# Values as the stationary operand of the attention's second product, for two query tiles at once, with feature-major results, weights spread through DRAM and merges behind the late gate

## The chip, the cores and the metric

The kernel runs on one core of a Trainium2 chip. TensorE (PE) multiplies; each multiplication has a weight load (PEld) that puts its stationary operand into the array, and a matmul that streams its moving operand through. VectorE (DVE), ScalarE (ACT) and GpSimd (POOL) do the elementwise work, and SyncE (SP) issues nearly all transfers. The metric is device time in microseconds: 1720.42 us is the median of three runs before (1719.05 to 1720.85).

## The reference, cut to what matters

One decoder block on a sequence of 1024 tokens of width 1024:

```
h = rms_norm(x);  z = h @ w_in            # q, k, v, GLU input, two gates
for each of 3 groups (dilation 1, 4, 16), 8 heads of 64:
    s = q k^T / 8 + bias(distance), masked to a causal window of 128 steps
    o_g = softmax(s) v;   lse_g = logsumexp(s)
y_attn = (sum over g of softmax_g(lse) * o_g) @ w_attn_out
y_conv = silu(layer_norm(conv31(glu))) @ w_conv_out
x += rms_norm((sig(ga) * y_attn + sig(gc) * y_conv) @ w_mix_out)
x += rms_norm(swiglu(rms_norm(x)))
```

The change concerns the second product of the attention (softmax weights times values) and the merge of the three groups with softmax weights over lse.

## The kernel before, in words

All products are done in three passes over a high and a low part of each operand: hi*hi, hi*lo, lo*hi. A float32 tile is split by a cast on ACT (high part) and a subtraction on DVE or POOL (low part).

**Order of the stages** (times of the profiled execution). Up to 112 us: normalisation and the first GLU blocks. From 112 to 551 us: `winograd` (lines 326 to 361) does 23 pairs of channel blocks, each as seven products with weight combinations A11, A12, S1 to S4 and A22, in the order A11, A12, S2, S1, S3, S4, A22. `prod` (lines 314 to 324) emits a product: 12 matmuls on lines 321 (hi*hi), 322 (hi*lo) and 323 (lo*hi), and one tick after each three. The bank X collects A11, S2, S3 and A22; lines 335, 340 and 345 copy banks out on ACT between the products, and a product that adds onto a bank follows the copy. `quarters` (lines 199 to 234) makes the combinations at fixed ticks of the pair, its parts c = 0 to 5: `both` (lines 193 to 197) casts on ACT (195) and subtracts on POOL (196); c = 1 and 3 add on POOL (215, 216, 222, 223); c = 4 splits S3/S4 with `both`; c = 5 casts on ACT (231) and subtracts on POOL (232) for A22. Line 706 adds up finished convolution channels on POOL, lines 650 to 695 are the convolution on DVE and POOL. From 551 us: the value projections `v` (lines 925 to 966, matmuls 948, 950, 952), and beside them the normalisation of the convolution. From 616 to 870 us the attention runs beside them, then beside the late gate (`plain_gate` with job `late`) and the first conv-out units (lines 1507 to 1526). Then the rest of conv-out, the attention output projection, the mix product (line 1585), and the FFN, whose first product is again `winograd` and whose second is line 1856.

**How the attention is interleaved.** `attention` is a generator. `beat`, called after each matmul of the stages beside it, adds RATE (0.42 beside the values, 0.8 beside late gate and conv-out) and advances the generator for each whole credit. One step s does `att_s` (first product and bias of query tile s), `att_e` (exponential of s-1), `att_t` (transposes of s-LT with the identity, then high and low copies on ACT and DVE), and `att_p` (second product of s-LP). There are 96 steps: 12 pairs of heads by 8 query tiles. `tick` advances background generators (`merge`, `conv_split`, `out_parts`, conv_norm) that say by `yield n` how many ticks to skip. Instructions stand on every engine and on the SP queue in the order in which this Python emits them, and every engine works in that order.

**The second product.** `att_p` holds the transposed weights stationary, high then low part, and streams the values: 128 columns (high and low part, line 1107), then 64 (high part, line 1109), for each key block and head. A DVE reduction (line 1115) adds the two halves into a token-major tile O. Groups 0 and 1 store O to DRAM; group 2 keeps it.

**The merge.** One for each pair of heads: two loads, the softmax over the groups, three multiplications by weights that DVE reads spread over 64 columns, two additions, and eight transposes on PE (line 1166) to feature-major. The first two merges run beside the value projections and go through DRAM (`out_parts`); the last two wait until the attention is done.

**Buffers.** SBUF tiles come from rings of buffers with a tag: 42 slots of 4 KB a partition (tag b), 11 halves of 2 KB (c), 3 ring tiles (d). A tile takes a buffer whose former tile is released, and its first write waits for that tile's last reader. Which buffer a tile gets is settled when the program is built, and the slots are used by all stages.

Of the kernel before, what the change touches and what calls it, by code (L numbers as in the profile page):

```python
# [9 lines left out]
F32 = mybir.dt.float32  # L10
# [36 lines left out]
NSLOT = 42  # L47

NRING = 3
NHALF = 11  # L50
# [12 lines left out]
class Build:  # L63
# [359 lines left out]
    def consts(self):  # L423
        nc = self.nc
        self.ident = self.small.tile([128, 128], F32, name="ident")
        nc.gpsimd.dma_start(self.ident, self.p_ident)
        tab = self.small.tile([33, 24], F32, name="tab")
        nc.gpsimd.memset(tab[32:33, :], 1.0)
        nc.gpsimd.dma_start(tab[0:32, :], self.p_tab)
        self.tab = tab  # L430
        self.mean_col = self.small.tile([128, 1], F32, name="mean_col")
# [457 lines left out]
    def others(self, hp):  # L889

        outs = [self.slot(), self.slot()]
        for i, o in enumerate(outs):
            self.nc.sync.dma_start(o.rearrange("p (u e) -> p u e", u=8),
                                   self.d_att[i, hp].rearrange("(p u) e -> p u e", u=8))
        return outs

# [19 lines left out]
    def value_parts(self, x, i):  # L916

        v = self.slot(F32R)
        d = v.rearrange("p (t e c) -> p t e c", t=8, e=2)
        y = x[:, i * H:(i + 1) * H].rearrange("p (t c) -> p t c", t=8)  # L920
        self.nc.scalar.copy(d[:, :, 0], y)
        self.nc.gpsimd.tensor_tensor(d[:, :, 1], y, f(d[:, :, 0]), op=OP.subtract)
        return v
# [45 lines left out]
    LT, LP = 3, 4  # L969
# [3 lines left out]
    def attention(self):  # L973
# [10 lines left out]
        while s < total + self.LP:  # L984
            if s < total:
# [22 lines left out]
                if u in (3, 4):  # L1008
                    if len(V) < 2:
                        V.append(self.value_parts(x, u - 3))  # L1010
                    if u == 4:
                        x = None
# [15 lines left out]
            if 0 <= s - self.LT < total:  # L1028
                self.att_t(live[s - self.LT])
                yield 0  # L1030
            if 0 <= s - self.LP < total:
                yield from self.att_p(live.pop(s - self.LP))
# [44 lines left out]
    def att_t(self, a):  # L1077

        nc = self.nc
        nb = len(a["blocks"])  # L1080
        ps = self.bank("t")
        for hh in range(2):
            for kb in range(nb):
                i = hh * nb + kb
                nc.tensor.transpose(ps[:, i * 128:(i + 1) * 128],  # L1085
                                    a["sp"][:, hh * 256 + kb * 128:hh * 256 + (kb + 1) * 128], self.ident)
        a["sp"] = None
        n = 2 * nb * 128
# [3 lines left out]
        a["pt"] = hi, lo  # L1092

    def att_p(self, a):

        nc = self.nc
        g, hp, u, nb = a["g"], a["hp"], a["u"], len(a["blocks"])
        ps = self.bank("o")
        hi, lo = a["pt"]
        for hh in range(2):  # L1100
            o = hh * 128
            for i, kb in enumerate(a["blocks"]):
                kb = self.place(g, kb)
                c = (kb % 4) * 256 + hh * 128
                v = a["V"][kb // 4]
                s = slice((hh * nb + i) * 128, (hh * nb + i + 1) * 128)
                nc.tensor.matmul(ps[:, o:o + 128], hi[:, s], v[:, c:c + 128], start=i == 0, stop=False,  # L1107
                                 skip_group_check=True)
                nc.tensor.matmul(ps[:, o:o + 64], lo[:, s], v[:, c:c + 64], start=False, stop=i == nb - 1,  # L1109
                                 skip_group_check=True)  # L1110
            yield 0
        if u == 0:
            self.O = self.ring() if g < 2 else self.slot()
        w = self.place(g, u)
        nc.vector.tensor_reduce(self.O[:, w * 128:(w + 1) * 128].rearrange("p (h c) -> p h c", h=2),
                                ps[:, :256].rearrange("p (h e c) -> p h c e", h=2, e=2), AX.X, OP.add)
        if u == 7:
            if g < 2:
                self.tokens_out(g, self.d_att[g, hp], self.O.rearrange("p (u e) -> p u e", u=8))
            else:  # L1120
                self.merges.append(self.bg(self.merge(hp, a["p"][4], self.O)))
            self.O = None

    def merge(self, hp, st, last):


        nc = self.nc

        late = 1 + (hp > 1)
        while hp > 1 and (self.fine is not None or hp > len(self.OT) + 2):  # L1130
            yield 0
        O = [*self.others(hp), last]
        last = None
        yield 1 + late
        t = self.tiny(96, "mrg", 2)
        m, r = (t[:, i * 16:(i + 1) * 16].rearrange("p (u e) -> p u e", u=8) for i in range(2))
        w = t[:, 48:].rearrange("p (g u e) -> p g u e", g=3, u=8)
# [3 lines left out]
        nc.scalar.activation(t[:, 48:], t[:, 48:], AF.Exp, scale=-1.0)  # L1141
        yield late
# [3 lines left out]
        nc.vector.tensor_tensor(w, w, r.unsqueeze(1).to_broadcast([128, 3, 8, 2]), op=OP.mult)  # L1146
        for g in range(3):
            y = O[g].rearrange("p (u h c) -> p u h c", u=8, h=2)
            a = w[:, g].unsqueeze(3).to_broadcast([128, 8, 2, 64])
            nc.vector.tensor_tensor(y, y, a, op=OP.mult)  # L1150
            yield late
        nc.vector.tensor_tensor(O[1], O[1], O[2], op=OP.add)
        O[2] = y = a = None
        yield late
        nc.vector.tensor_tensor(O[0], O[0], O[1], op=OP.add)
        O[1] = None
        yield 2 + 2 * late
        if hp < 2:
            hi = self.slot()
        else:  # L1160
            hi, lo = self.slot(F32R), self.slot(F32R)
        for h in range(2):
            ps = self.bank("t")
            for i in range(4):
                u = h * 4 + i
                nc.tensor.transpose(ps[:, i * 128:(i + 1) * 128], O[0][:, u * 128:(u + 1) * 128], self.ident)
            y = ps.rearrange("p (u m) -> p u m", u=4)
            a = hi.rearrange("p (m u) -> p u m", u=8)[:, h * 4:h * 4 + 4]
            nc.scalar.copy(a, y)
            if hp > 1:  # L1170
                nc.vector.tensor_tensor(lo.rearrange("p (m u) -> p u m", u=8)[:, h * 4:h * 4 + 4], y, f(a),
                                        op=OP.subtract)
            ps = y = a = None
            yield late
        if hp > 1:
            self.OT[hp] = hi, lo
        else:
            self.nc.sync.dma_start(self.d_ot[hp], hi)

    def out_parts(self):  # L1180

        for hp in range(2):
            x = self.slot()
            self.nc.sync.dma_start(x, self.d_ot[hp])
            yield 11
            self.OT[hp] = self.both(x)
            x = None
# [67 lines left out]
    def conv_split(self):  # L1255
# [11 lines left out]
        for i in range(16):  # L1267
# [3 lines left out]
            yield 3 if i < 5 else 1  # L1271
            while i == 5 and self.hH is not None:
                yield 0
# [71 lines left out]
def build(ctx, tc, aps):  # L1345
# [40 lines left out]
    B.d_att = {(g, hp): B.dram.tile([T, 128], F32, name=f"datt{g}{hp}") for g in range(2) for hp in range(4)}  # L1386
    B.d_v = {(g, hp): B.dram.tile([T, 128] if g else [128, T], F32, name=f"dv{g}{hp}") for g in range(3) for hp in range(4)}
    B.d_ot = [B.dram.tile([128, 1024], F32, name=f"dot{p}") for p in range(2)]
# [118 lines left out]
    for n, hf in [(0, 0), (1, 0), (0, 1), (1, 1)] + [(n, hf) for n in range(2, 8) for hf in range(2)]:  # L1507
# [20 lines left out]
    B.finish(op)  # L1528
# [443 lines left out]
```

## Time and profile before

| | |
|---|---|
| median of three runs | 1720.42 us |
| profiled execution | 1720.29 us |
| its span, first to last instruction | 1718.5 us |
| granted TensorE clock, mean | 0.999 |
| PE / PEld / DVE / ACT / POOL busy | 1700.9 / 1449.9 / 1235.5 / 794.2 / 461.4 us |
| moved by DMA | 277.03 MB, mean 161 GB/s |
| share of PE in the chain that ended last | 95% |

A profile row names the line, engine, operation and the tiles as out<-in without buffer numbers: p is a PSUM bank, b a slot, c a half, d a ring tile, others are DRAM tensors. Matmuls overlap, so their durations add up to more than their time; the distance from start to start is what one costs in a stream. In a timeline row stand the start, the length, and in brackets the idle time before it and what ended that. In a row of waits stand the total, the number and the longest.

### The profile page before, as it was taken

To read this page: it belongs to the slowest core of one execution; us is meant where nothing else is said; L and a number is where in the kernel's file an instruction comes from. 1 tells how busy PE (TensorE), PEld (TensorE's weight loads), DVE (VectorE), ACT (ScalarE), POOL (GpSimd) and SP (SyncE) were. 2 spreads that over 40 slices of the span, in tenths; PEclk is the share of its full clock that TensorE was granted. 3 is DMA by queue.
4 is the path that set the end of the run, shared out by engine and by line. 5 is a ranking of instruction groups with operands and counts; after the bars stand their busy time and mean duration, and the time that the engine had idled before them with its cause. 6 is when DMAs were issued, how large, how long until landed. Compare 5 with 4: busy or idle time off the path is not lost.

```text
span 1718.5 us, 24444 instructions
## 1 busy us (share of the span) xinstructions
PE 1700.9 (99%) x8698; PEld 1449.9 (84%) x8698; DVE 1235.5 (72%) x2217; ACT 794.2 (46%) x1552; POOL 461.4 (27%) x337
## 2 busy tenths in 40 slices
PE   8999999999999999999999999999999999999998
PEld 7788888888888999999888888888888888888886
DVE  6789978888998566686764855676556555677586
ACT  6344343444344486667722445633333333454463
POOL 0017777887886133342300120000000000000000
PEclk9999999999999999999999999999999999999999
DMA  4252433455568798888845732123222322494234
GB/s 165 103 183 86 151 125 132 152 189 172 172 177 215 214 276 209 243 225 232 277 170 182 257 113 98 68 74 132 108 92 92 127 94 92 145 361 156 97 136 153
DMA packets 169334, 277.03 MB, mean 161 GB/s; under 512 B 51921, under 2 KB 87244, under 8 KB 169212
## 3 DMA queue, kind: packets, MB, share of 16 engines
q1 hardware_dynamic: 168812, 274.97, 49.4%
q8 instruction: 68, 1.11, 0.3%
q14 instruction: 54, 0.44, 0.1%
q10 hardware_dynamic: 288, 0.27, 0.0%
q0 software_dynamic: 112, 0.24, 0.0%
HBM read 184.81 MB, written 95.33 MB: 163 GB/s over the span
## 4 chain that ended last, share of the span: by engine, by line
PE 95%; DMA 2%; ACT 1%; DVE 1%; POOL 1%; issue 0%; DVEq 0%; SPq 0%; ACTq 0%; POOLq 0%
PE p L321 16%; PE p L322 16%; PE p L323 15%; PE p L1856 12%; PE p L305 5%; PE p L309 5%; PE p L307 5%; PE p L1585 5%; PE p L950 2%; PE p L952 2%; PE p L948 2%; PE p L554 2%; PE p L1050 2%; PE p L1085 2%; PE p L1109 1%; PE p L1107 1%
## 5 line engine op out<-in xcount | busy, mean ns | idle before, releaser
L321 PE MATMUL p<-b,b 128*128 128x512 f32 x1204 | 469.1, 390 | 0.3 <-ACT c L340 0.3
L323 PE MATMUL p<-b,b 128*128 128x512 f32 x1204 | 469.0, 390 | 0.0
L322 PE MATMUL p<-b,b 128*128 128x512 f32 x1204 | 468.9, 389 | 0.0
L321 PEld LDWEIGHTS p<-b,b 128*128 128x128 f32 x1204 | 226.1, 188 | 48.1 <-ACT c L340 0.7
L323 PEld LDWEIGHTS p<-b,b 128*128 128x128 f32 x1204 | 226.1, 188 | 46.7
L322 PEld LDWEIGHTS p<-b,b 128*128 128x128 f32 x1204 | 226.1, 188 | 46.6
L1856 PE MATMUL p<-b,b 128*128 128x512 f32 x924 | 209.6, 389 | 0.0
L1856 PEld LDWEIGHTS p<-b,b 128*128 128x128 f32 x924 | 173.5, 188 | 35.9
L684 DVE SCALAR_TENSOR_TENSOR p<-b,par,p 128x511 f32<-128x511 f32 (+14 forms) x232 | 163.5, 739 | 0.0
L305 PE MATMUL p<-b,b 128*128 128x512 f32 x368 | 147.7, 401 | 0.0
L309 PE MATMUL p<-b,b 128*128 128x512 f32 x368 | 146.4, 398 | 0.0
L307 PE MATMUL p<-b,b 128*128 128x512 f32 x368 | 146.2, 397 | 0.0
L195 ACT CAST b<-d 128x1024 fp32r<-128x1024 f32 x86 | 90.4, 1051 | 105.1 <-POOL d L216 55.0
L196 POOL TENSOR_TENSOR b<-d,b 128x1024 fp32r<-128x1024 f32 x44 | 106.8, 2428 | 79.9 <-ACT b L195 72.5
L196 DVE TENSOR_TENSOR b<-d,b 128x1024 fp32r<-128x1024 f32 x42 | 51.3, 1221 | 101.0 <-ACT b L195 101.0
L948 PE MATMUL p<-b,b 128*128 128x256 f32 x384 | 115.5, 301 | 0.0
L950 PE MATMUL p<-b,b 128*128 128x256 f32 x384 | 114.8, 299 | 0.0
L952 PE MATMUL p<-b,b 128*128 128x256 f32 x384 | 114.7, 299 | 0.0
L1193 DVE TENSOR_TENSOR b<-c,b 128x512 fp32r<-128x512 f32 x101 | 71.0, 704 | 38.2 <-ACT b L1192 38.0
L1193 DVE TENSOR_TENSOR b<-b,b 128x512 fp32r<-128x512 f32 x117 | 80.1, 690 | 20.7 <-ACT b L1192 18.8
L1192 ACT CAST b<-b 128x512 fp32r<-128x512 f32 x117 | 72.3, 620 | 45.7 <-PE p L1856 18.0
L1585 PE MATMUL p<-b,b 128*128 128x512 f32 x384 | 89.4, 392 | 0.0
(229 smaller groups left out, 3092.4 us busy)
## 6 DMA issues: line engine op xcount, KB each, us to landing
b<-w_in SPq DMA_DIRECT2D x30, 512.0 KB, 4.9
dk<-c SPq DMA_DIRECT2D x48, 256.0 KB, 2.9
dq<-c SPq DMA_DIRECT2D x48, 256.0 KB, 3.7
b<-dq SPq DMA_DIRECT2D x48, 256.0 KB, 5.9
b<-dk SPq DMA_DIRECT2D x48, 256.0 KB, 6.6
b<-w_fi SPq DMA_DIRECT2D x24, 512.0 KB, 4.9
d<-w_in SPq DMA_DIRECT2D x23, 512.0 KB, 4.0
dqS<-c SPq DMA_DIRECT2D x44, 256.0 KB, 2.1
```

The costliest lines, as they stand in the source:

```text
L196: self.wsplit.tensor_tensor(lo, x, f(hi), op=OP.subtract)
L305: nc.tensor.matmul(ps, hi[:, s], a, start=kt == 0, stop=False)
L307: nc.tensor.matmul(ps, hi[:, s], b, start=False, stop=False)
L309: nc.tensor.matmul(ps, lo[:, s], a, start=False, stop=kt == nk - 1)
L321: nc.tensor.matmul(ps, hi[:, s], a, start=first and kt == 0, stop=False, skip_group_check=True)
L322: nc.tensor.matmul(ps, hi[:, s], b, start=False, stop=False, skip_group_check=True)
L323: nc.tensor.matmul(ps, lo[:, s], a, start=False, stop=kt == 3, skip_group_check=True)
L684: nc.vector.scalar_tensor_tensor(A[i][:, j:], src[i][:, :H - j], w[i], A[i][:, j:], op0=OP.mult, op1=OP.add)
L948: nc.tensor.matmul(o, a, hi[:, s], start=kt == 0, stop=False)
L1193: nc.vector.tensor_tensor(s[:, 512:512 + n], src, f(s[:, :n]), op=OP.subtract)
L1585: nc.tensor.matmul(banks[tt][nh], st, wt[:, nh * H:(nh + 1) * H], start=bool(kt == 0 and a), stop=bool(kt == KT - 1 and b))
L1856: nc.tensor.matmul(acc[t], x, y, start=first and e == 0, stop=last and e == 2, skip_group_check=True)
```

## The change

`att_p` makes the values stationary (64 features and 2 columns more, 66 in all) and streams the transposed weights of two neighbouring query tiles: three matmuls (value high by weight high, value low by weight high, value high by weight low) into one half of a PSUM bank, 256 columns where both tiles attend the block, 128 where one does. The result is feature-major, so DVE copies replace the reductions and all three groups store O to DRAM. A small tile `vx` holds the low part of the last value block. `att_t` transposes for two tiles and one head at a time; LT and LP go from 3 and 4 to 4 and 5. The merge writes its softmax weights to DRAM, loads them spread over 64 partitions (`spread`), multiplies feature-major and splits into parts; its transposes, `out_parts` and `others` go. Merges wait until the input activations are freed (after the late gate) and go one after another (`turn`). `conv_split` waits for the late gate after its fourth split instead of its sixth. The banks for conv-out are taken as soon as the attention is done. Slots go from 42 to 41, halves from 11 to 12.

```diff
-NSLOT = 42
+NSLOT = 41
-NHALF = 11
+NHALF = 12
...
+        self.vx = [self.small.tile([128, 66], F32R, name=f"vx{i}") for i in range(4)]
...
+        w = self.vx[self.vi % 4]
+        self.vi += 1
+        self.nc.gpsimd.tensor_copy(w[:, :64], f(d[:, 7, 1]))
+        return v, w
...
-    LT, LP = 3, 4
+    LT, LP = 4, 5
...
+    def att_t(self, live, k):
+        a, b, hh = live[k & ~1], live[k | 1], k & 1
+        items = [(a, u), (b, u), (a, u - 1), (b, u + 1)]
+        items = [(x, x["blocks"].index(kb)) for x, kb in items if kb in x["blocks"]]
+        ps = self.bank("t")
+        for j, (x, i) in enumerate(items):
+            c = hh * 256 + i * 128
+            nc.tensor.transpose(ps[:, j * 128:(j + 1) * 128], x["sp"][:, c:c + 128], self.ident)
...
+    def att_p(self, live, k):
+        if g == 2:
+            todo = [(u, 0, 128, 0), (u + 1, 128, 128, 128)]
+        else:
+            n = 256 + 128 * (len(a["blocks"]) > 1)
+            todo = [(u, 0, 256, 0)] + [(u - 1, 256, 128, 0)] * (n > 256) + [(u + 1, n, 128, 128)]
+        for j, (kb, x, n, q) in enumerate(todo):
+            vh = v[:, c:c + 66]
+            vl = v[:, c + 64:c + 130] if c < 896 else w
+            o = ps[0:66, hh * 256 + q:hh * 256 + q + n]
+            for i, (y, z) in enumerate(((vh, hi), (vl, hi), (vh, lo))):
+                nc.tensor.matmul(o, y, z[:, x:x + n], ...)
+            if j < 2:
+                yield 0
...
+        for h in range(2):
+            x = ps[0:64, h * 256:(h + 1) * 256]
+            nc.vector.tensor_copy(d[h * 64:(h + 1) * 64], x if g < 2 else ...)
+        if u == 6:
+            nc.sync.dma_start(self.d_att[g, hp], self.O)
...
+    def spread(self, hp, g):
+        x, d = self.slot(), self.d_w[hp]
+        for e in range(2):
+            self.nc.sync.dma_start(x[e * 64:(e + 1) * 64], bass.AP(
+                tensor=d.tensor, offset=d.offset + (2 * g + e) * T, ap=[[0, 64], [1, T]]))
+        return x
...
+        nc.sync.dma_start(self.d_w[hp].rearrange("f (p u) -> p f u", u=8), ...)
+        yield 6
+        while self.hH is not None or hp > self.turn:
+            yield 0
+        y, x = load(0), self.spread(hp, 0)
+        yield 1
+        z, w = load(1), self.spread(hp, 1)
+        yield 8
+        nc.vector.tensor_tensor(y, y, x, op=OP.mult)
...
+        self.turn += 1
...
+        self.OT[hp] = self.both(y)
...
-            yield 3 if i < 5 else 1
-            while i == 5 and self.hH is not None:
+            yield 3 if i < 3 else 1
+            while i == 3 and self.hH is not None:
...
-        if B.tags["g"] == 2 and B.fine is None and not any(e in B.gens for e in B.merges):
+        if B.tags["g"] == 2 and B.fine is None:
             B.banks(g=6, s=2)
-        if n == 4 and hf == 0:
-            op = B.bg(B.out_parts())
```

More of the change, by code (lines that the diff above doesn't have):

```diff
@@ L1028, in attention @@
             if 0 <= s - self.LT < total:
-                self.att_t(live[s - self.LT])
+                self.att_t(live, s - self.LT)
                 yield 0
             if 0 <= s - self.LP < total:
-                yield from self.att_p(live.pop(s - self.LP))
+                yield from self.att_p(live, s - self.LP)
             s += 1
@@ L1091, in att_t @@
         nc.vector.tensor_tensor(lo[:, :n], ps[:, :n], f(hi[:, :n]), op=OP.subtract)
-        a["pt"] = hi, lo
-    def att_p(self, a):
+        a["pt", hh] = hi, lo
+    def att_p(self, live, k):
         nc = self.nc
[L1097 to L1107, printed above, removed]
-                                 skip_group_check=True)
-                nc.tensor.matmul(ps[:, o:o + 64], lo[:, s], v[:, c:c + 64], start=False, stop=i == nb - 1,
-                                 skip_group_check=True)
-            yield 0
-        if u == 0:
[L1113 to L1121, printed above, removed]
-            self.O = None
@@ L1124, in merge @@
-    def merge(self, hp, st, last):
-        nc = self.nc
[L1129 to L1135, printed above, removed]
+        a, b, hh = live[k & ~1], live[k | 1], k & 1
+        g, hp, u = a["g"], a["hp"], a["u"]
+        if hh == 0:
+            a["o"] = self.bank("o")
+        ps = a["o"]
+        hi, lo = a.pop(("pt", hh))
@@ L1156, in merge @@
[L1156 to L1187, printed above, removed]
+        nc.vector.tensor_tensor(t[:, 96:].rearrange("p (g e u) -> p g u e", g=3, e=2).rearrange("p g u e -> p g u e"), w,
+                                r.unsqueeze(1).to_broadcast([128, 3, 8, 2]), op=OP.mult)
@@ new lines, in merge @@
+        yield 8
+        nc.vector.tensor_tensor(y, y, x, op=OP.mult)
+        x = None
+        x = self.spread(hp, 2)
+        yield 2
+        nc.vector.tensor_tensor(z, z, w, op=OP.mult)
+        w = None
+        w = load(2)
+        yield 2
+        nc.vector.tensor_tensor(y, y, z, op=OP.add)
+        z = None
+        self.turn += 1
+        yield 6
+        nc.vector.tensor_tensor(w, w, x, op=OP.mult)
+        x = None
+        yield 2
+        nc.vector.tensor_tensor(y, y, w, op=OP.add)
@@ L1189, in split @@
+        w = None
+        yield 2
+        self.OT[hp] = self.both(y)
+    turn = 0
     def split(self, src, n):
```

83 lines of the change are left out of this document (48 added, 35 removed).

## The prediction

> **What bounds the kernel now.** I read the page's shares first, then the windows by stage, then the timeline of single matmuls. Three stages matter here: the seven-product stage (112 to 551 us, lines 314 to 361), the attention beside the value projections and the first conv-out units (613 to 870 us), and what follows.
>
> ```profile
> PE 1700.9 (99%) x8698; PEld 1449.9 (84%) x8698; DVE 1235.5 (72%) x2217; ACT 794.2 (46%) x1552; POOL 461.4 (27%) x337
> ...
> 112.00:550.80 438.80, 438.53 (x1934) 362.68 (x1933) 387.53 (x534) 182.72 (x271) 337.28 (x192) 1.00 0.49 152
> ...
> 613.00:802.70 189.70, 187.78 (x1622) 186.88 (x1622) 135.21 (x469) 128.65 (x412) 70.20 (x88) 1.00 0.86 236
> 802.70:870.00 67.30, 64.98 (x429) 57.29 (x427) 47.80 (x167) 45.09 (x151) 19.06 (x22) 1.00 0.75 233
> ```
>
> The columns are the stretch and its length, then busy PE, weight loads, DVE, ACT, POOL, the granted clock, DMA share and GB/s. PE is busy throughout. So a saved PE step comes off the end one for one, and a new PE wait is added one for one. In the attention weight loads are as busy as the matmuls (186.88 of 189.70 us). In the seven-product stage POOL is busy 337 of 439 us, more than anywhere else: 14.7 us of each pair's 19.1 (23 pairs of channel blocks).
>
> What one step of the second product costs:
>
> ```profile
> 720.07 0.28 PE L950 MATMUL p<-b,b 128*128 128x256 f32 x1
> 720.19 0.22 PE L1107 MATMUL p<-b,c 128*128 128x128 f32 x1
> 720.25 0.25 PE L1109 MATMUL p<-b,c 128*128 128x64 f32 x1
> 720.33 0.37 PE L952 MATMUL p<-b,b 128*128 128x256 f32 x1
> 720.53 0.28 PE L948 MATMUL p<-b,b 128*128 128x256 f32 x1
> 720.65 0.28 PE L950 MATMUL p<-b,b 128*128 128x256 f32 x1
> ```
>
> Start to start is the cost, since ends overlap. A 256-column matmul takes 0.12 us (720.53 to 720.65). From 720.07 to 720.53 there are two of those and one pair of lines 1107 and 1109: the pair takes 0.46 - 0.24 = 0.22 us. Its 128 columns stream in 0.06 us (720.19 to 720.25) and its 64 columns cannot take longer, so the pair is bound by two weight loads of about 0.112 us, not by its columns.
>
> **The change, part by part. Second product.** Before: 280 pairs x 0.224 = 62.7 us, which is also the busy time of line 1107's group:
>
> ```profile
> L1107 PE MATMUL p<-b,c 128*128 128x128 f32 x280 | 62.7, 250 | 0.3 <-DVE b L1115 0.3
> ...
> L459 PEld LDWEIGHTS p<-b,tab x6: 82/84/86, 52.1 to 92.2; 33*8 33x8 f32 x6
> ...
> L1107 PEld LDWEIGHTS p<-b,c x280: 186/190/193, 618.8 to 869.6; 128*128 128x128 f32 x140
> ```
>
> After, the values are stationary: 66 columns instead of 128, three matmuls per key block and two query tiles. Counting att_p over 12 head pairs and both heads gives 192 matmuls of 256 columns and 456 of 128 (152 triples). The 256s cost 0.12 each, 23.0 us. For the 128s the unknown is a 66-column load. Loads of 8 and of 128 columns last 84 and 190 ns: 0.88 ns per column, so 66 columns save 55 ns of the 112 and about 57 are left, under the 60 ns that 128 columns stream. Only the 128-column load of the matmul behind each triple is exposed: 60 + 60 + 112 = 232 ns, 152 x 0.232 = 35.3 us. Sum 58.3, a gain of **4.4 us**. Bounds: all 456 at 60 ns gives 50.4 (gain 12.3); all at 112 ns gives 74.1 (loss 11.4). I stay near the first, since the 8-column row shows that loads shrink with columns.
>
> [...]
>
> **Transposes.** att_t keeps its 280 transposes, only grouped by two tiles. The merge's 32 go:
>
> ```profile
> 888.59 0.44 PE p L1166 x4
> ```
>
> Eight groups of four at 0.44 us: **-3.5 us**. Their copies, the 96 reductions on DVE (0.42 us each) against 96 copies from PSUM, the 24 POOL copies of 64 columns and the extra column of merge work lie on engines that are at most 71% busy in the attention (135 of 190 us). They cost nothing there while PE's order has one step of slack between att_t and att_p, which the change keeps (LT 4, LP 5). If that cover goes, the price is the late-gate term below.
>
> **The slot.** NSLOT falls from 42 to 41, and NHALF rises from 11 to 12. Slots are taken by weights, splits and spills in every stage, not in the attention alone. In both built programs the live slots reach the pool's size in the seven-product stage, so there a tile is written into the buffer that was freed last. I laid the buffers of the changed program beside the times of this trace. In 10 of the 23 pairs, the low half of S3/S4 (quarters, c = 4, POOL line 196) gets the buffer that held the high half of S1/S2. Its last reader is the second-to-last matmul (line 322) of the S1 product, and the very next product is S3. One such pair:
>
> ```profile
> 365.09 1.05 ACT L195 CAST b<-b 128x1024 fp32r<-128x1024 f32 x1 [1.98 <-PE p L322]
> ...
> 368.67 0.62 ACT L231 CAST b<-b 128x512 fp32r<-128x512 f32 x1 [2.52 <-POOL b L196]
> 369.19 0.58 ACT L340 COPY c<-p 128x512 f32<-128x512 f32 x1
> ```
>
> ```profile
> 366.23 2.41 POOL L196 TENSOR_TENSOR b<-b,b 128x1024 fp32r<-128x1024 f32 x1 [1.42 <-ACT b L195]
> ```
>
> ```profile
> 370.03 0.39 PE L322 MATMUL p<-b,b 128*128 128x512 f32 x1
> 370.26 0.39 PE L323 MATMUL p<-b,b 128*128 128x512 f32 x1
> 370.48 0.39 PE L321 MATMUL p<-b,b 128*128 128x512 f32 x1
> 370.71 0.39 PE L322 MATMUL p<-b,b 128*128 128x512 f32 x1
> 370.94 0.39 PE L323 MATMUL p<-b,b 128*128 128x512 f32 x1
> ```
>
> Now POOL writes from 366.23 to 368.64, and PE reads the low half at 370.94: 2.3 us to spare. Changed, POOL may start at 370.03 + 0.39 = 370.42, ends at 372.83, and the matmul of 370.94 waits **1.9 us**. ACT stands in line too: line 231's buffer is freed by line 323 at 370.65, its cast and then line 340's copy of the X bank end at about 371.8, and the S3 product, which adds onto that bank, can start only then (370.48 before). That lies inside the 1.9. Ten pairs: 19 us.
>
> What is behind POOL's waiting instruction: lines 232, 196, 215, 216, 706, 196, 222, 223 and the next 196. The row 368.67 shows that ACT's line 231 already waits on that last one for a buffer. The pair after 218 us:
>
> ```profile
> 222.33 1.30 POOL L215 TENSOR_TENSOR d<-b 128x512 f32<-128x512 f32 x1
> 223.71 1.28 POOL L216 TENSOR_TENSOR d<-d,d 128x512 f32<-128x512 f32 x1
> 224.96 2.40 POOL L706 TENSOR_TENSOR b<-b,b 128x1024 f32<-128x1024 f32 x1
> 227.43 2.40 POOL L196 TENSOR_TENSOR b<-d,b 128x1024 fp32r<-128x1024 f32 x1
> 229.79 1.30 POOL L222 TENSOR_TENSOR b<-d,b 128x512 f32<-128x512 f32 x1
> 231.04 1.30 POOL L223 TENSOR_TENSOR b<-d,d 128x512 f32<-128x512 f32 x1
> 233.50 2.41 POOL L196 TENSOR_TENSOR b<-b,b 128x1024 fp32r<-128x1024 f32 x1 [1.16 <-ACT b L195]
> ```
>
> ```profile
> 217.71 0.39 PE L322 MATMUL p<-b,b 128*128 128x512 f32 x1
> ...
> 237.20 0.39 PE L321 MATMUL p<-b,b 128*128 128x512 f32 x1
> ```
>
> POOL starts at 218.10 and runs 2.41 + 1.30 + 2.40 + 1.30 + 1.28 + 2.40 to 229.2. A cast of 1.05 (its buffer is the one line 706 frees), 2.40, 1.30, 1.30, a cast, 2.41: 238.8, where now it is 235.9. Lines 231 and 340 after it end at 240.0; PE, already 1.9 late, is ready at 237.20 + 1.9 = 239.1. So this pair waits 0.9 us more. In seven pairs the buffers give such a wait (0.7 to 1.2 each): I take 1.0, 7 us. Together **+26 us** for the slot. Bounds: 0, if POOL's buffers turn out otherwise; 42, if POOL's 4.2 us of delay in each of the ten reached PE whole. I take the sum of the rows.
>
> In the FFN's second product the same shortage makes 31 first writes wait about 2.2 us:
>
> ```profile
> L1856 PE MATMUL p<-b,b 128*128 128x512 f32 x924 | 209.6, 389 | 0.0
> ```
>
> A split is issued three steps of 12 matmuls ahead, 36 x 209.6 / 924 = 8.2 us, so I price this at nothing. Were that lead used up, each would cost up to 2.2.
>
> **Late gate, loads and merges.** conv_split now holds after its fourth split, and merges start only when hH is freed. So after the late gate four splits stand together, and the eighth's load is issued behind the gate's store:
>
> ```profile
> 828.86 0.34 SPq L1439 DMA_DIRECT2D dgc<-b  x1
> 829.30 1.20 SPq L1262 DMA_DIRECT2D c<-dact  x2
> ...
> 842.11 0.62 ACT L1192 CAST b<-c 128x512 fp32r<-128x512 f32 x1 [2.58 <-DMA c<-dact]
> ...
> PE p L1050 <- DMA b<-dk: 1.6, 2, 1.1
> ...
> PE p L321 <- ACT c L340: 0.3, 1, 0.3
> ...
> c<-dact SPq DMA_DIRECT2D x16, 256.0 KB, 10.0
> dgc<-c SPq DMA_DIRECT2D x14, 256.0 KB, 2.5
> ```
>
> A DMA of that size lands after 2.5 (gates, stored) to 10 us (these loads). ACT waits in order at that split, and behind it stand attention's exponentials and high-half copies, on which PE waits. Bounds 0 (landed within the slack of one step) and 8; I take **+3**, the size of the wait at 842. The merges add 24 spread loads of 256 KB and four more tile loads and stores; SP sends them between the loads for the last group (b<-dk, c<-rep), so part of the +3 is theirs. By its yields a merge passes the turn every 17 ticks from the first conv-out tick on, so the fourth does at 68 and has its parts at about 82 of the 128 ticks: the attention output projection does not wait. If it had to, the price would be the rest of that merge.
>
> **Sum.** The profiled execution is 1720.29 us (span 1718.5), 0.13 under the median of the three runs. 1720.3 - 4.4 - 3.5 + 26 + 3 = 1741.4.
>
> **Rivals.** *Other side, faster:* the seven-product stage hides the slot. It decides at one point: if the low half's buffer is free 2.3 us earlier, before 368.5 in the pair shown, POOL is done when PE asks. Then 1720.3 - 7.9 + 0 to 3 = 1712 to 1716. For it: POOL is idle 4.4 us per pair. Against it: the idle time stands before the wait and cannot be drawn forward past a buffer that PE holds. *Loads do not shrink:* 456 at 112 ns; +11.4 in place of -4.4 gives 1757. Against it stands the 84 ns row. *The late-gate burst and the spread loads keep the last group waiting:* +8 to +13 instead of +3, 1746 to 1752; for it the 1.1 us wait on b<-dk, against it a DMA share of only 0.75 in the stretch from 802.70.
>
> **How the numbers follow.** My forecast, slower by 12 to 28, has 0.78. The burst rival has 0.06, the loads rival 0.06, and faster 0.08. No change within 0.2% (3.4 us, about what a measurement here can tell) needs the slot to cost just 3 to 8 us: 0.02. Low end: 19 for the slot and nothing for the burst, 1732. High end: slot 28, burst 10, or part of the loads rival: 1754. That leaves the faster case and the loads rival outside.
>
> **What would show it.** In the changed trace, 112 to 551 us should be about 26 us longer with the same matmuls. POOL line 196 would be ended by PE line 322 in about ten places, and PE lines 321 and 323 would wait on ACT line 340 and POOL line 196, where now the one wait is the 0.3 us quoted above. From 613 to 829 us it should be about 7 us shorter, with triples of 232 ns. The prediction is wrong if that first stage keeps its length, or if the 66-column loads follow each other at 110 ns.

## The result and the profile after

The changed kernel takes **1765.91 us** (median; 1765.19 to 1772.44), the kernel before, run beside it, 1720.58 us: a ratio of **1.0274 (95%: 1.0249 to 1.0299)**. It is slower, as forecast, but by 45 us and not by 21: 12 us above the upper end of the range. The profiled execution took 1765.19 us, with a span of 1763.3 us.

The first view is the page's share of busy time, after the change.

```profile
PE 1711.0 (97%) x8754; PEld 1441.2 (82%) x8754; DVE 1253.7 (71%) x2215; ACT 787.1 (45%) x1546; POOL 467.2 (26%) x365
```

PE was busy 99% of a shorter span before, so it now waits. Where, the windows by stage tell (stretch, length, busy PE, weight loads, DVE, ACT, POOL, granted clock, DMA share, GB/s). The stages are the seven products, the attention beside the values, and the stretch from the last value matmul to the attention's end. After:

```profile
112.00:583.20 471.20, 448.82 (x1932) 362.36 (x1931) 392.80 (x536) 182.37 (x272) 336.60 (x192) 0.99 0.46 141
646.30:831.70 185.40, 181.78 (x1657) 180.00 (x1655) 131.00 (x458) 125.72 (x412) 70.52 (x104) 1.00 0.85 230
831.70:913.20 81.50, 70.78 (x460) 57.30 (x459) 62.70 (x179) 44.31 (x147) 21.55 (x28) 0.94 0.87 238
```

The last two stages before (the first is the prediction's row from 112.00, 438.80 us):

```profile
613.80:802.70 188.90, 186.98 (x1616) 186.08 (x1615) 135.21 (x469) 128.06 (x412) 70.20 (x88) 1.00 0.86 236
802.70:869.90 67.20, 64.88 (x428) 57.19 (x426) 47.80 (x167) 45.09 (x151) 19.06 (x22) 1.00 0.75 233
```

So the 44.9 us between the two profiled executions are +32.4 in the seven products, -3.5 in the attention beside the values, +14.3 from there to its end, and +1.7 in all the rest.

**The seven products.** PE's waits from 112 to 583 us, after (total, times, longest):

```profile
PE p L321 <- ACT c L340: 18.2, 16, 1.9
PE p L323 <- POOL b L196: 4.2, 10, 0.4
```

Before, the only wait of this kind was 0.3 us. The pair that the prediction worked out now stands at 384 us. Its matmuls:

```profile
384.67 0.39 PE L322 MATMUL p<-b,b 128*128 128x512 f32 x1
384.90 0.39 PE L323 MATMUL p<-b,b 128*128 128x512 f32 x1
386.48 0.50 PE L321 MATMUL p<-b,b 128*128 128x512 f32 x1 [1.19 <-ACT c L340]
386.82 0.40 PE L322 MATMUL p<-b,b 128*128 128x512 f32 x1
387.63 0.50 PE L323 MATMUL p<-b,b 128*128 128x512 f32 x1 [0.41 <-POOL b L196]
387.97 0.40 PE L321 MATMUL p<-b,b 128*128 128x512 f32 x1
```

and POOL's subtraction, after:

```profile
385.21 2.36 POOL L196 TENSOR_TENSOR b<-b,b 128x1024 fp32r<-128x1024 f32 x1 [4.22 <-PE p L322]
```

POOL sits idle for 4.22 us until line 322 has read the buffer, then takes 2.36 us, and PE reads the low half at 387.63. From 384.90 to 387.97 four matmuls took 3.07 us; at 0.23 each, as in the prediction's rows, they would take 0.92. The pair lost 2.15 us, of which the brackets show 1.60. Idle time understates: in the stream a matmul starts 0.23 us after the one before it, which lasts 0.39, so each of the two waits also loses that overlap of 0.16, and from the matmul behind it to the next start are 0.34 us and not 0.23.

**The second product** moves as the forecast has it. A stretch of it after (x3 is a triple):

```profile
752.73 0.34 PE L1123 MATMUL p<-c,b 128*66 128x128 f32 x3
752.90 0.33 PE L949 MATMUL p<-b,b 128*128 128x256 f32 x1
753.08 0.28 PE L951 MATMUL p<-b,b 128*128 128x256 f32 x1
753.19 0.28 PE L947 MATMUL p<-b,b 128*128 128x256 f32 x1
753.31 0.34 PE L1123 MATMUL p<-c,b 128*66 128x128 f32 x3
```

From 752.73 to 753.31 are a triple and three 256-column matmuls of 0.12: 0.58 - 0.36 = 0.22 us, where I had 0.232. The extra sits behind line 949 (0.18 instead of 0.12); that the wide load of the next matmul is no longer hidden there is my reading of it. The 66-column loads last 136 ns (median, from start to end), close to the straight line between the prediction's 84 ns for 8 columns and 190 ns for 128.

**The end of the attention.** ACT, after, waits here for loads of conv_split:

```profile
861.50 0.62 ACT L1219 CAST b<-c 128x512 fp32r<-128x512 f32 x1 [2.71 <-DMA c<-dact]
...
878.14 0.62 ACT L1219 CAST b<-c 128x512 fp32r<-128x512 f32 x1 [3.07 <-DMA c<-dact]
878.66 0.37 ACT L1095 CAST c<-p 128x256 fp32r<-128x256 f32 x1
...
883.75 0.62 ACT L1219 CAST b<-c 128x512 fp32r<-128x512 f32 x1 [3.17 <-DMA c<-dact]
```

Directly behind the split of 878.14 stands line 1095, the copy of transposed weights that PE is waiting for:

```profile
879.08 0.34 PE L1123 MATMUL p<-c,b 128*66 128x128 f32 x2 [1.77 <-ACT c L1095]
```

The waits of PE and of ACT in this stretch, after:

```profile
PE p L1123 <- DVE c L1096: 5.9, 9, 1.5
PE p L1123 <- ACT c L1095: 4.6, 2, 2.9
...
ACT b L1219 <- DMA c<-dact: 11.9, 5, 3.2
```

Before, ACT's waits on c<-dact were 4.0 us. The queue of SP, after, shows why the loads are late:

```profile
861.56 1.46 SPq L876 DMA_DIRECT2D b<-dk  x2
863.33 0.40 SPq L1187 DMA_DIRECT2D b<-datt  x1
864.28 1.10 SPq L1155 DMA_DIRECT2D b<-dw  x2
866.27 0.33 SPq L1289 DMA_DIRECT2D c<-dact  x1
867.56 0.38 SPq L480 DMA_DIRECT2D c<-rep  x1
870.30 0.32 SPq L1187 DMA_DIRECT2D b<-datt  x1
871.29 1.66 SPq L1155 DMA_DIRECT2D b<-dw  x2
875.49 0.33 SPq L1289 DMA_DIRECT2D c<-dact  x1
```

Line 1187 and line 1155 are the first merge's loads (512 KB, and twice 256 KB); conv_split's loads (line 1289) are issued between them. SP itself stood for 4.5 us ahead of two of conv_split's loads, and by the profile a load of the merge ended both waits:

```profile
SPq L1289 <- DMA b<-datt: 4.5, 2, 2.5
```

### The profile page after: what moved, and what is told of

It is laid out like the page before. It is cut to its first block, busy times and chain, and to the rows that moved or that the text cites. A ratio compares the mean times of both kernels' runs of the same rounds, so it can differ in the third digit from the quotient of the medians.

```text
span 1763.3 us, 24468 instructions
## 1 busy us (share of the span) xinstructions
PE 1711.0 (97%) x8754; PEld 1441.2 (82%) x8754; DVE 1253.7 (71%) x2215; ACT 787.1 (45%) x1546; POOL 467.2 (26%) x365
## 4 chain that ended last, share of the span: by engine, by line
PE 82%; POOL 6%; DMA 5%; ACT 3%; DVE 2%; issue 1%; SPq 0%; DVEq 0%; POOLq 0%; ACTq 0%
PE p L321 14%; PE p L323 14%; PE p L322 14%; PE p L1880 12%; PE p L1609 4%; PE p L305 4%; PE p L309 4%; PE p L307 4%; POOL b L196 3%; PE p L1123 2%; PE p L557 2%; PE p L1050 2%; PE p L949 2%; PE p L947 2%; PE p L951 2%
## 5 line engine op out<-in xcount | busy, mean ns | idle before, releaser
L321 PE MATMUL p<-b,b 128*128 128x512 f32 x1204 | 472.0, 392 | 18.2 <-ACT c L340 18.2
L323 PE MATMUL p<-b,b 128*128 128x512 f32 x1204 | 470.9, 391 | 4.2 <-POOL b L196 4.2
L322 PE MATMUL p<-b,b 128*128 128x512 f32 x1204 | 469.9, 390 | 0.0
L1880 PE MATMUL p<-b,b 128*128 128x512 f32 x924 | 210.2, 389 | 0.9 <-ACT b L1219 0.7
L305 PE MATMUL p<-b,b 128*128 128x512 f32 x368 | 147.4, 401 | 0.0
L309 PE MATMUL p<-b,b 128*128 128x512 f32 x368 | 146.5, 398 | 0.6 <-DVE b L189 0.6
L307 PE MATMUL p<-b,b 128*128 128x512 f32 x368 | 146.2, 397 | 0.0
L947 PE MATMUL p<-b,b 128*128 128x256 f32 x384 | 112.8, 294 | 0.0
L951 PE MATMUL p<-b,b 128*128 128x256 f32 x384 | 112.2, 292 | 0.0
L949 PE MATMUL p<-b,b 128*128 128x256 f32 x384 | 112.1, 292 | 0.0
L1123 PE MATMUL p<-c,b 128*66 128x128 f32 (+1 forms) x620 | 89.2, 243 | 11.2 <-DVE c L1096 5.9
L1219 ACT CAST b<-c 128x512 fp32r<-128x512 f32 x101 | 62.2, 618 | 76.1 <-PE p L1880 24.2
```

The source lines that it names most:

```text
L305: nc.tensor.matmul(ps, hi[:, s], a, start=kt == 0, stop=False)
L307: nc.tensor.matmul(ps, hi[:, s], b, start=False, stop=False)
L309: nc.tensor.matmul(ps, lo[:, s], a, start=False, stop=kt == nk - 1)
L321: nc.tensor.matmul(ps, hi[:, s], a, start=first and kt == 0, stop=False, skip_group_check=True)
L322: nc.tensor.matmul(ps, hi[:, s], b, start=False, stop=False, skip_group_check=True)
L323: nc.tensor.matmul(ps, lo[:, s], a, start=False, stop=kt == 3, skip_group_check=True)
```

## Experiments

Two theories stand behind the prediction. *Slot:* one slot fewer in the seven-product stage costs the first term, whatever the attention does. *Late gate:* the second term is the burst behind the late gate; for this there are two rivals, the four splits that now stand together, and the merges' loads. Times are medians; the kernel before took 1719.9 to 1720.7 us beside these runs.

**One slot taken away, nothing else.** The kernel before holds one slot through the seven products.

```diff
+    park = B.slot()                       # ahead of the first pair of the stage
+    nc.vector.memset(park[:, 0:1], 0.0)
...
+    nc.vector.memset(park[:, 0:1], 0.0)   # after the last pair
+    park = None
```

> The kernel before, with one of its 42 slots held by an idle tile from the first pair of the seven-product stage to its end; nothing else differs. Theory: the lost slot alone makes that stage longer, because ten low halves of S3/S4 get the buffer that the high half of S1/S2 leaves; the stage grows from 438.8 us by 30 to 33 us, the rest stays, total 1750 to 1754. Rival: the stage grew through something else of the change (halves, memsets, new tiles), and this kernel stays within 3 us of 1720.6.

Measured: 1753.85 us, ratio 1.0194 (1.0176 to 1.0211). PE's waits from 112 to 583 us in this run:

```profile
PE p L321 <- ACT c L340: 18.2, 16, 1.9
PE p L323 <- POOL b L196: 4.2, 10, 0.4
```

They are those of the changed kernel, to the tenth. The stage takes 471 us here too, and the total is inside the expected 1750 to 1754. The slot is the first term, and nothing of the attention's change belongs to it.

**All of the change with 42 slots.** To fit, the second product takes 64 columns and no `vx`, there are 11 halves, and LT and LP are 3 and 4.

```diff
-NSLOT = 41
+NSLOT = 42
...
-NHALF = 12
+NHALF = 11
...
-    LT, LP = 4, 5
+    LT, LP = 3, 4
...
-            vh = v[:, c:c + 66]
-            vl = v[:, c + 64:c + 130] if c < 896 else w
+            vh = v[:, c:c + 64]
+            vl = v[:, c + 64:c + 128]
...
-        t = self.tiny(144, "mrg", 2)
+        t = self.tiny(144, "mrg", 1)
```

> The changed kernel with 42 slots again. Room for them is made by 64 instead of 66 columns (which needs no extra tile for the last value block), 11 halves with LT and LP 3 and 4, and one buffer for the merge's small tile. Slot theory: the seven-product stage is back at 439 us and the total at 1731 to 1736. Rival (the stage is long for another reason): 1763 to 1768. If 64 columns or the shorter lead cost something in the attention, the first stage is short and the stretch from 551 us longer than in the changed kernel.

Measured: 1722.37 us, ratio 1.0013 (1.0004 to 1.0023), 43.5 us under the changed kernel. The seven-product stage is back at 438.8 us, as expected of the slot; the total lies 9 us below the expected 1731 to 1736, so this run gives back more than the slot. The next two stages in this run:

```profile
614.00:794.70 180.70, 180.28 (x1656) 179.57 (x1655) 132.08 (x454) 123.63 (x407) 66.51 (x88) 1.00 0.85 234
794.70:872.40 77.70, 69.42 (x459) 56.48 (x459) 60.87 (x183) 45.27 (x152) 18.69 (x22) 0.93 0.86 249
```

The attention beside the values gains 8.2 us (188.9 to 180.7), and the stretch behind gives 10.5 back (67.2 to 77.7). The loss in the stretch stays without the slot. That the attention gains 8.2 here and 3.5 in the changed kernel this run cannot put down to one thing, as slots, halves, columns and lag change together.

**The wide operand.** Is the second product bound by its loads, as the 232 ns say?

```diff
-            vh = v[:, c:c + 64]
-            vl = v[:, c + 64:c + 128]
-            o = ps[0:64, hh * 256 + q:hh * 256 + q + n]
+            vh = v[:, c:c + 128]
+            vl = v[:, c:c + 128]
+            o = ps[:, hh * 256 + q:hh * 256 + q + n]
```

> The kernel of the run with 42 slots (1722.4 us), with all 128 columns of the values as the stationary operand of each matmul of the second product instead of 64 (the low half's own product is left out and the high half's is made twice, so the number of matmuls and their columns stay, and the output is another). Theory (the second product is bound by its weight loads; a load's time goes with its columns): each of the 152 triples of 128 streamed columns takes 3 x 112 = 336 ns instead of 232: 15.8 us slower than that run, 1735 to 1741 us. Rival (the columns streamed set the pace, and the loads are hidden whatever their width): no change, 1720 to 1725 us.

Measured: 1735.10 us, 12.7 more than with 64 columns, at the low end of what was expected. The same stage in this run:

```profile
614.50:807.60 193.10, 192.02 (x1655) 191.25 (x1654) 133.83 (x454) 125.46 (x409) 65.95 (x88) 1.00 0.81 222
```

It is 12.4 us longer than with 64 columns, and matmul by matmul the run is 15 us behind the one with 64 columns at 826 us: the loads set the pace, and their time goes with the columns. One of 128 columns lasts 193 ns in this run (mean), one of 64 columns 136 ns in the run with 42 slots.

**The splits, and then the merges.** First the hold after the fourth split, alone in the kernel before:

```diff
-            yield 3 if i < 5 else 1
-            while i == 5 and self.hH is not None:
+            yield 3 if i < 3 else 1
+            while i == 3 and self.hH is not None:
```

> The kernel before, with one edit: conv_split holds after its fourth split instead of its sixth. Theory A (the splits alone make the burst): 4 to 10 us slower, 1725 to 1731 us, with PE waits on ACT and DVE between 829 and 870 us. Theory B (the merges make it): within 2 us of the kernel before.

Measured: 1723.31 us, ratio 1.0020 (1.0011 to 1.0030): 3.2 us, between the two expectations. The stretch is 69.5 us instead of 67.2, with one wait of 2.1 us on ACT and a granted clock of 0.95 in the mean of the stretch (1.00 before). The splits' price is the prediction's +3, but it is not the 10 to 14. Then the reverse, the hold after the sixth split in the kernel with 42 slots:

> The kernel of the run with 42 slots (1722.4 us), with conv_split holding after its sixth split again instead of after its fourth; the merges still start behind the late gate. That run gained 8.7 us up to the late gate and gave 10.5 back between 826 and 865 us. Theory A (the four splits that stand together behind the late gate, with their copies, subtractions and loads, hold up the last group's copies): with two splits fewer there most of the 10.5 goes, 1712 to 1717 us. Theory B (the merges' loads and multiplies, which start in the same stretch, hold them up): the 10.5 stays, 1720 to 1725 us.

Measured: 1721.65 us, ratio 1.0008 (0.9999 to 1.0018), 0.7 us less than with the hold after the fourth. ACT's waits for conv_split's loads in the stretch, in this run (10.5 us with the hold after the fourth):

```profile
ACT b L1213 <- DMA c<-dact: 11.6, 3, 5.0
```

The burst theory in its form "splits" has fallen: with two splits fewer there ACT waits as long. The merges are left. They may hold up more than conv_split: PE's longest wait in this stretch, 4.6 us ahead of the attention's first product (line 1044), ended by the profile with a load of the merge (b<-datt).

**Merges after the attention.** In the changed kernel (`fine` is the attention as long as it runs):

```diff
-        while self.hH is not None or hp > self.turn:
+        while self.hH is not None or self.fine is not None or hp > self.turn:
```

> The changed kernel, with the merges waiting until the attention is done as well as for the late gate. Theory that the merges' loads and DVE work beside the last attention steps cost most of the 14 us between late gate and the attention's end: 8 to 12 us less than the changed kernel, 1754 to 1758. Rival, that the four splits behind the late gate (ACT waiting for their load) cost them: 0 to 4 us less, 1762 to 1766. A loss instead of a gain would say that the four merges no longer fit in the 100 ticks that are left.

Measured: 1776.07 us, 10 us slower than the changed kernel: the loss that was named as the sign that four merges no longer fit there. The stretch does shrink from 81.5 to 71.5 us, and the attention ends 5.5 us earlier (907.7 instead of 913.2 us), but then PE waits in a new place, on line 189 for 11.5 us, which I had not expected. The same edit with 42 slots and the hold after the sixth split:

> As the one before, and conv_split holds after its sixth split as in the kernel before, and the merges wait until the attention is done. If slot, splits and merges are the whole of the loss, what is left is the gain of the second product and the transposes: 1712 to 1718, faster than the kernel before. If the attention keeps a cost of its own (DVE copies, DMA), 1720 to 1728.

Measured: 1730.80 us, ratio 1.0065 (1.0050 to 1.0080), above both expectations. Matmul by matmul this run is about 10 us ahead of the kernel before until that one's 904 us, and then loses 19.6. PE's waits behind the attention, with 42 slots:

```profile
PE p L309 <- DVE b L189: 14.6, 3, 6.1
```

and what DVE does there, in the same run:

```profile
916.13 1.22 DVE L1192 TENSOR_TENSOR b<-b,b 128x1024 f32<-128x1024 f32 x1 [6.55 <-DMA b<-dw]
917.27 0.74 DVE L1541 SCALAR_TENSOR_TENSOR b<-p,par,b 128x512 f32<-128x512 f32 x1
917.93 0.68 DVE L189 TENSOR_TENSOR b<-b,b 128x512 fp32r<-128x512 f32 x1
```

A merge's multiply (line 1192) is issued 12 ticks after its spread load and holds DVE for 6.55 us until it lands. Soon behind it stands line 189, the split of the conv-out weights that PE needs next. It is the same mechanism as on ACT, on another engine. With six ticks more in both places:

```diff
-        yield 8
+        yield 14
...
-        yield 6
+        yield 12
```

> The kernel of the run with 42 slots, hold after the sixth split and merges that wait for the end of the attention (1730.8 us), with six ticks more between a merge's loads and the multiplies that need them, at both places. That run was 9.8 us ahead of the kernel before at the end of the attention and then lost 18 us where the splits of the weights (line 189) stood on DVE behind multiplies that waited for their loads. Theory (it is the distance from load to multiply): PE's wait on line 189 falls from 14.6 us to under 4, 1712 to 1718 us, faster than both kernels. Rival (the DMA engines are full in that stretch, so loads that are given more time only pile up): the waits stay, 1725 to 1732 us.

Measured: 1728.64 us. The wait on line 189 is gone altogether, but the expected time did not come. PE's longest wait in this run, and two stretches behind the attention:

```profile
PE p L305 <- ACT b L195: 11.8, 1, 11.8
...
872.00:900.00 28.00, 28.00 (x125) 23.18 (x124) 17.18 (x19) 4.48 (x7) 0.00 (x0) 1.00 1.03 319
900.00:950.00 50.00, 37.01 (x151) 29.50 (x150) 26.79 (x30) 9.73 (x15) 1.15 (x1) 0.87 1.03 330
```

The DMA share is 1.03 from 872 to 950 us, where the merges run, and the fourth merge is done about 12 us after the attention output projection asks for it. Both theories were half right: distance cures the wait on DVE, but there is no room for four merges behind the attention.

**Merges behind conv_split's loads.** The room is ahead of that: in the last run the DMA share was 0.60 from 830 to 850 us and 0.41 from 850 to 872. The first merge starts 12 ticks after `hH` (the input activations) is freed, and merges that run behind the attention get six ticks more between load and multiply, in the kernel with 42 slots and the hold after the sixth split:

```diff
         while self.hH is not None or hp > self.turn:
             yield 0
+        if hp == 0:
+            yield 12
+        far = 0 if self.fine is not None else 6
...
-        yield 8
+        yield 8 + far
...
-        yield 6
+        yield 6 + far
```

> The kernel of the run with 42 slots and hold after the sixth split (1721.65 us), with the first merge started 12 ticks after hH is freed instead of at once, so that its loads are issued behind conv_split's last ones instead of between them; merges that run after the end of the attention get six ticks more between load and multiply. Theory (it is the order of the loads on SP's queue: the merges' 512 and 256 KB loads ahead of conv_split's, whose copies hold up ACT and with it the attention): ACT's waits on c<-dact fall from 11.6 us to under 3, the attention ends at 859 to 865 us instead of 873.9, the fourth merge is done before the output projection asks for it, and the time is 1709 to 1716 us, faster than both kernels. Rival (the attention has no room for a merge at all, whenever it starts): the attention ends at 868 us or later, 1718 to 1724 us.

Measured: **1709.95 us, ratio 0.9947 (0.9931 to 0.9962)**: faster than both kernels, 56 us under the changed one (six of seven runs took 1709.7 to 1711.2 us, one 1719.0). The three stages in this run:

```profile
112.10:550.90 438.80, 438.52 (x1934) 362.56 (x1933) 387.59 (x534) 182.69 (x271) 337.39 (x192) 1.00 0.49 152
613.80:794.90 181.10, 180.42 (x1656) 179.57 (x1655) 132.02 (x454) 123.42 (x407) 66.38 (x88) 1.00 0.85 233
794.90:861.50 66.60, 64.78 (x459) 53.64 (x458) 57.05 (x180) 45.23 (x153) 18.36 (x22) 1.00 0.82 251
```

and ACT's wait for conv_split's loads:

```profile
ACT b L1216 <- DMA c<-dact: 0.2, 1, 0.2
```

From 11.6 us to 0.2, and the stretch from 78.2 to 66.6 us. The merge's loads are still issued beside the attention, only behind conv_split's, and the stretch moves more per us than in the changed kernel (251 GB/s against 238), so a higher rate of transfer alone does not make the waits. The edit moves the loads in order and in time at once; the two were not tried apart. The same edit in the changed kernel, with its 41 slots and its hold after the fourth split:

> The changed kernel (1765.9 us; 41 slots, hold after the fourth split) with one edit: the first merge starts 12 ticks after hH is freed instead of at once, and merges after the attention get six ticks more between load and multiply. Theory (the 14 us of the late gate's stretch come from the merges' loads ahead of conv_split's, in the changed kernel as in the one with 42 slots, where this edit brought 11.7 us): 10 to 14 us faster than the changed kernel, 1752 to 1756 us, with the seven-product stage still at 471 us. Rival (with 41 slots the merges start late anyway, for want of buffers): within 3 us of the changed kernel.

Measured: 1758.05 us, 7.9 less than the changed kernel: above the rival's 3 and short of the 10 to 14 that were expected. The stretch takes 71.1 us instead of 81.5 and ACT waits 2.5 us on c<-dact instead of 11.9, so the stretch itself gave back 10.4 us. Stages ahead of it, which the edit does not touch, took 5.7 of that in the profiled execution: a wait of 2.3 us at 663 us that ends with a transfer, and a lower granted clock: 0.993 in the mean of the execution against 0.995 in the changed kernel's, though the stretch itself has 0.98 against 0.94. What is left above the 67.2 of before, 3.9, is near the 3.2 of the splits.

**One step more between scores and second product.** In the faster kernel, LT 4 and LP 5:

> The same kernel, and besides the transposes and second products one step later (LT 4, LP 5, as in the changed kernel). Theory (the attention's remaining waits are copies that are late by less than one step): 0 to 4 us faster than with 3 and 4. Rival (one more step holds half tiles longer, and they run out): 0 to 6 us slower.

Measured: 1719.16 us, 9.2 more. Of the 7.8 between the two profiled executions, 5.4 are in the attention beside the values (186.5 instead of 181.1 us), where PE now waits on line 1090 in six places (1.7 us) and for loads (b<-dk) in two (2.5 us), and 2.9 are in the stretch behind. The rival held, and beyond its upper end: the copies of line 1089, which write half tiles, wait for their reader, line 1117, 21.6 us in 22 places instead of 8.3 in 6. And the changed kernel with 3 and 4 and its 12 halves:

> The changed kernel with LT 3 and LP 4 instead of 4 and 5 (12 half buffers stay). Theory (one step more between scores and second product holds half buffers longer and makes the waits that cost the attention 4 us of its 8 us of gain; with 42 slots and 11 half buffers that step cost 9.2 us): 2 to 6 us faster than the changed kernel, 1760 to 1764 us. Rival (the twelfth half buffer pays for the longer lag): within 2 us, or slower, if copies are late.

Measured: 1765.79 us, no difference; the stage from 650.7 to 835.0 is 184.3 us long, against 185.4. The theory fell: with 12 halves the longer lag costs nothing that shows, with 11 it cost 9.2 us. That the changed kernel's twelfth half pays for its lag fits both, but the slots differ between the two pairs as well.

## Why the prediction was right or wrong

- **The slot, +26 us (bounds 0 to 42): right in mechanism and place, too small; measured +32.4.** The ten pairs are there, with sixteen waits on line 340 and ten on line 196 in the places that the buffers gave. Matched matmul by matmul with the kernel before, nine of the ten pairs cost 2.1 to 2.2 us each and not 1.9, since the overlap of the matmuls is lost as well; the tenth, at 450 us, costs 3.2 with a drop of the clock behind it (1.6 in the run with the first merge later, where the clock stays). That makes 21 without the drop. Six other places, not seven, cost 0.6 to 2.2 each without the clock, 8 in all instead of 7. A thing that the sum did not have took up to 3.4: the granted clock fell to 0.5 for 3.4 us twice in this stage.
- **Second product, -4.4, and transposes, -3.5: right in mechanism, and small; the changed kernel does not show all of it.** The triple costs 0.22 us. In the faster kernel, where little else disturbs it, the whole change is worth 10.6 us against 7.9 in the sum. In the changed kernel the attention beside the values gains only 3.5 of the 8.2 that it gains with 42 slots. Of these 4.7, 2.6 are PE's waits for loads (b<-dk). Such waits go with the longer lag: with 42 slots they are 2.5 us at LT 4 and LP 5 and none shows at 3 and 4, and with 41 slots and the shorter lag they are 0.7. But the shorter lag gave the stage only 1.1 us, with other waits in their place (1.3 on a DVE result, line 1053), so the rest stays open. With the slot parked the kernel before was not slower in this stage, but there the slot was free again by then.
- **Late gate, +3 us (bounds 0 to 8): the step that failed; measured +14.3.** The +3 was taken from the size of one wait for a split, and the merges' loads were said to be "part of the +3". The splits alone do cost 3.2 us. What was missing is the merges' loads among conv_split's on SP's queue: in the two places shown a merge puts 1 MB ahead of the next conv_split load, ACT waits at that split, and the attention's exponentials and copies stand behind it on ACT. With the first merge's loads behind conv_split's the stretch is 11.6 us shorter with 42 slots, and 10.4 with 41. The rival of +8 to +13 named this stretch and the spread loads; I gave it 0.06 because the DMA share there was 0.75, an average over 67 us that says nothing of the order in the queue. Even its +13 was below what came. Of the measured 14.3, up to 5.1 are again the clock (10.2 us at 0.5).
- **The merge's end, priced at nothing by ticks (the fourth merge done at 82 of 128): right for the changed kernel,** whose output projection does not wait. The price for the other case was real: 11.8 us in the run with merges after the attention and six ticks more.
- **FFN's second product, 0: nearly right.** PE waits there for 0.7 us on ACT and 0.2 on DVE, and is 1.5 us later behind it. The +1.7 of all the rest has this in it, and the saved transposes behind the attention against it.
- **The range** ended at 1754 with "slot 28, burst 10, or part of the loads rival". Slot 28 and burst 10 alone add up to 1750. The slot came to 32 with its clock drops, the burst to 14, and of the gain of 7.9 only 3.5 showed in its stage. No term held the clock, which may have taken up to 3.4 and 5.1 of the two.

## What to carry to other kernels

A buffer less in a shared ring is priced in the stage whose live tiles fill the ring, not in the stage that is changed: lay the buffers of the new program beside the old times and look for writes that wait for the matmul just before. An average DMA share does not say that a load will be in time; read the queue as it is filled, and ask which engine stands in line behind the instruction that needs the load. Work that is put off needs a place with room: with 42 slots the same four merges cost some 12 us at once behind the gate, 19.6 after the attention, and nothing that shows 12 ticks later.

## What the hardware showed beside this

The granted clock of the changed kernel is 0.50 in four stretches of its profile (ahead of the last microseconds): they begin at 409.4, 453.8, 863.4 and 880.5 us and last 3.4 us each, the third 6.8. Two views of the same pair of the seven products, the 3.41 us with the stall and the 3.41 us behind them, first the changed kernel:

```profile
450.39:453.80 3.41, 1.79 (x7) 1.04 (x7) 2.41 (x4) 3.03 (x5) 3.32 (x2) 1.00 0.66 236
453.80:457.21 3.41, 3.41 (x10) 2.63 (x9) 2.51 (x5) 0.14 (x1) 3.33 (x3) 0.50 0.46 129
```

then the changed kernel with the first merge later, which has the same code there:

```profile
450.69:454.10 3.41, 1.92 (x7) 1.31 (x8) 2.38 (x4) 3.09 (x5) 3.41 (x2) 1.00 0.70 249
454.10:457.51 3.41, 3.41 (x17) 2.80 (x16) 3.41 (x5) 0.42 (x1) 3.33 (x3) 1.00 0.38 105
```

In the first, PE is idle for 1.62 us of the 3.41, and behind that the clock is 0.50, with 10 matmuls in 3.41 us. In the second it is idle for 1.49 us, the clock stays at 1.00, and 17 matmuls follow in the same time. So the stretch at 0.50 costs an estimated 1.7 us (half of 3.41) beside the stall itself. Why the clock fell behind the one and not behind the other, the runs do not show. In the faster kernel's three stages the clock is 1.00 throughout, and 0.999 in the mean of the execution.
